# Modulation sums moved from TensorE to VectorE, ScalarE and GpSimd in a two-layer token trunk

## The chip, the core and the metric

The kernel runs on one core of one Trainium2 chip. The metric is the device time of one execution in microseconds (us). Three executions of the kernel before took 2267.44, 2270.04 and 2270.38 us, a median of 2270.04 us.

## The reference: what is computed

The trunk has two layers. Each layer runs a feed-forward sub-layer (FFN), a token-mixing block and a second FFN, over 256 latent rows and 256 context rows of width 1024. Each sub-layer s of each layer l is modulated by three vectors of 1024 numbers, a shift, a scale and a gate. They are products of SiLU(c) for latents, or SiLU(c_ctx) for context, with one column block of the weight `w_ada[l]` (1024 x 9216), plus a bias. The parts that matter here are:

```
def modulated_norm(xs, gain, mod, s):
    return rms_norm(xs, gain) * (1.0 + mod_vec(mod, 3 * s + 1)) + mod_vec(mod, 3 * s)

def gated_residual(xs, y, gain, mod, s, weight):
    return xs + weight * mod_vec(mod, 3 * s + 2) * rms_norm(y, gain)

def ffn_sublayer(xs, mod, s, g_pre, g_post, w_in_f, w_out_f):
    a, g = jnp.split(modulated_norm(xs, g_pre, mod, s) @ w_in_f, 2, axis=-1)
    return gated_residual(xs, (jax.nn.silu(a) * g) @ w_out_f, g_post, mod, s, MACARON_WEIGHT)
```

Only the latent rows leave the trunk. In the second layer the context rows therefore stop mattering after they have given keys, values and states to the mixing block: the gate of its mixing block and all three vectors of its second FFN are read for latents alone. The input x, c, ctx and all weights are float32.

## The kernel before: how the work is laid out

**Main products.** Each float32 operand is split in a high and a low part (`whi`/`wlo` for weights, `hThi`/`hTlo` for activations), and a product is three matmuls, L284 to L286. Weights come in tiles of 1 MB (`wraw`, two buffers). ScalarE copies each half of one into `whi` (L207), VectorE subtracts to get `wlo` (L210), and three such pairs are buffered. In the mixing block GpSimd takes over L210.

**An FFN** (`ffn`) has two parts. The input products run over 44 blocks of 24 matmuls of 512 columns. After a block ScalarE applies SiLU (L654), or VectorE multiplies (L658), ScalarE copies (L660) and VectorE subtracts (L661). The output products follow in `natural_out`. There are four FFNs. The first (layer 0), the second (layer 0, after mixing) and the third (layer 1) carry modulation work beside their input products. The fourth carries none.

**Modulation sums** (`Ada`). Before, a vector takes four chunks of 256 rows by 1024 columns of `w_ada` (1 MB each, L319), which lie in turn in two tiles, `adaG` and `aday`. A chunk is used by four float32 matmuls of 32 rows (L340), two for each of its two 128-row blocks, that go to four 32-row strips of one PSUM tile. After four chunks ScalarE copies the sums out (L346). For a shift or scale, four transposes (L291) and VectorE additions of the bias (L362 to L365) finish the vector. For a gate, four matmuls with a selection matrix `sel` (L381) join the partial sums, VectorE adds the bias and multiplies the gains (L383, L384), and a small DMA from GpSimd's queue writes it to DRAM (L387), from where `load_gate` spreads it over all rows.

**Order of work.** Instructions are emitted in program order into each engine's queue, and each engine runs its own queue in that order. Modulation work is a generator. The main code calls `tick` with a nominal time, twice per block with 2.6. The generator runs one step at a tick if its wake time has passed, and a step says when it wants to wake (`every`). In the three FFNs that carry it, the input products give 88 ticks. After the last block `finish(K, ada)` runs every step that is left, one after the other, before anything of the output products is emitted. Chunk DMAs stand on the queue of SyncE (SP), in one line with the loads of `wraw`, and the DMA of a chunk waits until its place has been read.

Of the kernel before, what the change touches and what calls it, by code (L numbers as in the profile page):

```python
# [297 lines left out]
def aux_tile(K):  # L298
    return K.ps_aux.tile([P, 512], F32, tag="aux", name="aux")


def t2k(K, name="t2k"):
    return K.tp.tile([P, 512], F32, tag="t2k", name=name)


class Ada:


    def __init__(self, K, places, jobs):

        self.K, self.places, self.jobs = K, places, jobs
        self.chunks = [(l, c, k) for l, s, kind, _ in jobs
                       for c in ((3 * s, 3 * s + 1) if kind == "norm" else (3 * s + 2,)) for k in range(0, 8, 2)]
        self.loaded = self.n = 0
# [8 lines left out]
    def run(self, every, bank=aux_tile):  # L323
        self.every, self.bank = every, bank
        self.pump()
        yield every[0]
        for l, s, kind, weight in self.jobs:
            yield from (self.norm(l, s) if kind == "norm" else self.gate(l, s, weight))

# [37 lines left out]

    def gate(self, l, s, weight):

        K, nc, v, q = self.K, self.K.nc, self.K.nc.vector, self.K.nc.gpsimd  # L370
        c0 = (3 * s + 2) * D
        ev = yield from self.sums()
        bp = t2k(K, "bp")
        v.memset(bp, 0.0)
        for st in range(2):
            nc.sync.dma_start(bp[st:st + 97:32, 0:256], K.b_ada[l, c0:c0 + D].rearrange("(q c) -> q c", q=4))
            nc.sync.dma_start(bp[st:st + 97:32, 256:512], K.norm_post[l, s].rearrange("(q c) -> q c", q=4))
        yield 8.0
        pt = self.bank(K)
        for k in range(4):  # L380
            nc.tensor.matmul(pt[32 * k:32 * k + 32, 0:256], K.sel[:, k // 2, :], ev[:, 256 * (k % 2):256 * (k % 2) + 256], start=True, stop=True,  # L381
                             tile_position=(0, 32 * k))
        v.tensor_tensor(out=ev[:, :256], in0=pt[:, :256], in1=bp[:, 0:256], op=OP.add)  # L383
        v.scalar_tensor_tensor(out=ev[:, :256], in0=ev[:, :256], scalar=weight, in1=bp[:, 256:512], op0=OP.mult, op1=OP.mult)  # L384
        gd = K.dr.tile([2, 4, 256], F32, tag=f"gd{l}{s}", name=f"gd{l}{s}")
        for st in range(2):
            q.dma_start(gd[st], ev[st:st + 97:32, :256])  # L387
        K.gd[l, s] = gd
# [232 lines left out]

def ffn(K, l, s, f, pn, tiles, nxt, jobs, every=(5.0, 7.6), pools=None, prep=False):
    nc = K.nc
# [7 lines left out]
    with pools.es as es:  # L631
        hb = None
        big = [gp.tile([P, 2, 1024], F32, tag=t, name="ada" + t) for t in ("G", "y1")]
        ada = add_task(K, Ada(K, big, jobs).run(every), 5.0)
        hid = lambda k, n: (ha[k][:, n, :] if n < 11 else hb[k][:, n - 11, :])
# [51 lines left out]
        G = gp.tile([P, 2, 1024], F32, tag="G", name="G")  # L687
        load_gate(K, l, s, G)
        y1 = gp.tile([P, 4, 512], F32, tag="y1", name="y1")
# [930 lines left out]
def trace(K, nc, tc, rec):  # L1620
# [4 lines left out]
    with ExitStack() as es:  # L1625
# [17 lines left out]
        K.sc = C([P, 8, 32], "sc")  # L1643
        K.sel = C([P, 2, 32], "sel")
        K.npT = C([P, 2, 3, 8], "npT")
# [13 lines left out]
        nc.scalar.activation(K.sc[:, :, 0:2], pt[:, 0:16].rearrange("p (s b) -> p b s", s=2), AF.Silu)  # L1659
        nc.vector.memset(K.sel, 0.0)  # L1660
        id4 = K.ident.rearrange("p (a b r) -> p a b r", a=2, b=2)
        nc.vector.tensor_tensor(out=K.sel[:, :, 0:2], in0=id4[:, 0, :, 0:2], in1=id4[:, 1, :, 0:2], op=OP.add)
        pt = aux_tile(K)
# [5 lines left out]
        for l in range(2):  # L1669
# [5 lines left out]
        ada = Ada(K, [h[:, 4 * j:4 * j + 4, :].rearrange("p (i a) b -> p i (a b)", i=2) for h in pools.hidden(F32) for j in range(2)],  # L1675
                  [(0, 0, "norm", None)])
        for i, _ in enumerate(ada.run((0.0, 0.0), mm_tile)):
# [24 lines left out]
        for l in range(2):  # L1702
            last = l == 1
            jobs = [(0, 0, "gate", 0.5), (0, 1, "norm", None), (0, 1, "gate", 1.0)] if l == 0 else []
            jobs.append((l, 2, "norm", None))
            if last:
                jobs.append((l, 2, "gate", 0.5))
            pn = ffn(K, l, 0, 0, pn, range(4), lambda: PreNorm(K, l, 1), jobs, (7.6, 7.6) if last else (5.0, 7.6), pools, True)
            pools = None
            pn = mix(K, l, pn, last, lambda: PreNorm(K, l, 2))  # L1710
            if last:
                ffn(K, l, 2, 1, pn, range(2), None, [])
            else:
                pn = ffn(K, l, 2, 1, pn, range(4), lambda: PreNorm(K, l + 1, 0), [(l, 2, "gate", 0.5)] + [(l + 1, i, *j) for i, w in ((0, 0.5), (1, 1.0)) for j in (("norm", None), ("gate", w))])

# [64 lines left out]
```

## Time and profile of the kernel before

| | |
|---|---|
| median of three executions | 2270.04 us |
| profiled execution | 2264.31 us, span 2262.5 us |
| mean granted TensorE clock | 0.982 |
| TensorE matmul busy | 2150.5 us (95%) |
| VectorE busy | 1123.5 us (50%) |
| ScalarE busy | 770.1 us (34%) |
| GpSimd busy | 400.0 us (18%) |
| DMA | 323.12 MB, mean 143 GB/s |

In the profile PE is TensorE's matmul side and PEld its weight loads. DVE is VectorE, ACT ScalarE, POOL GpSimd and SP SyncE. A line such as L340 is a line of the kernel before. Times are in us unless marked ns. Matmuls are pipelined, so the busy time of one is longer than the distance to the next, and the distance between starts is what counts. The profiled execution is 1.8 us longer than its span.

### The profile page before, as it was taken

To read this page: it belongs to the slowest core of one execution; us is meant where nothing else is said; L and a number is where in the kernel's file an instruction comes from. 1 tells how busy PE (TensorE), PEld (TensorE's weight loads), DVE (VectorE), ACT (ScalarE), POOL (GpSimd) and SP (SyncE) were. 2 spreads that over 40 slices of the span, in tenths; PEclk is the share of its full clock that TensorE was granted. 3 is DMA by queue.
4 is the path that set the end of the run, shared out by engine and by line. 5 is a ranking of instruction groups with operands and counts; after the bars stand their busy time and mean duration, and the time that the engine had idled before them with its cause. 6 is when DMAs were issued, how large, how long until landed. Compare 5 with 4: busy or idle time off the path is not lost.

```text
span 2262.5 us, 29051 instructions
## 1 busy us (share of the span) xinstructions
PE 2150.5 (95%) x11691; PEld 1731.5 (77%) x11691; DVE 1123.5 (50%) x2025; ACT 770.1 (34%) x1287; POOL 400.0 (18%) x372
## 2 busy tenths in 40 slices
PE   5899999989999999999999988999999889897998
PEld 3677778877777678777777876778887778787997
DVE  6883332357446655532332356733324675646554
ACT  3222222333532433422222332222223345344443
POOL 1660000022313110100000027500000243441000
PEclk8999999999999999999999998999999999998999
DMA  8566542333312122355554335633332553333554
GB/s 292 177 221 211 188 153 88 108 131 134 115 51 82 47 89 93 120 197 177 183 186 156 110 116 170 228 132 112 103 103 87 184 168 104 120 123 130 187 182 154
DMA packets 210910, 323.12 MB, mean 143 GB/s; under 512 B 15608, under 2 KB 152440, under 8 KB 210776
## 3 DMA queue, kind: packets, MB, share of 16 engines
q1 hardware_dynamic: 196736, 287.17, 38.1%
q0 software_dynamic: 9584, 31.56, 4.2%
q10 hardware_dynamic: 4456, 2.53, 0.4%
q8 instruction: 92, 1.51, 0.3%
q14 instruction: 42, 0.34, 0.0%
HBM read 307.57 MB, written 14.71 MB: 142 GB/s over the span
## 4 chain that ended last, share of the span: by engine, by line
PE 48%; DVE 5%; issue 1%; ACT 1%; POOL 1%; DMA 1%; ACTq 0%; SPq 0%; DVEq 0%; POOLq 0%
PE mm L284 15%; PE mm L285 14%; PE mm L286 14%; PE aux L340 2%; PE aux L291 1%; PE aux L1398 1%; DMA r_tq<-tab 1%; DVE wlo L210 1%; ACT jk L399 0%; DVE hThi L461 0%; PE aux L1548 0%; ACT h L458 0%; DVE hTlo L462 0%; DVE xs L432 0%; PE aux L1604 0%
## 5 line engine op out<-in xcount | busy, mean ns | idle before, releaser
L284 PE MATMUL mm<-hThi,whi 128*128 128x512 f32 (+1 forms) x1992 | 719.1, 361 | 8.4 <-DVE hThi L461 8.2
L285 PE MATMUL mm<-hTlo,whi 128*128 128x512 f32 (+1 forms) x1992 | 702.4, 353 | 7.5 <-POOL hTlo L462 7.1
L286 PE MATMUL mm<-hThi,wlo 128*128 128x512 f32 (+1 forms) x1992 | 700.0, 351 | 0.0
L210 DVE TENSOR_TENSOR wlo<-wraw,whi 128x1024 fp32r<-128x1024 f32 (+1 forms) x285 | 362.7, 1278 | 427.8 <-ACT whi L207 426.3
L284 PEld LDWEIGHTS mm<-hThi,whi 128*128 128x128 f32 x1992 | 381.3, 191 | 124.9 <-issue 54.5
L207 ACT ACTIVATE whi<-wraw 128x1024 fp32r<-128x1024 f32 (+1 forms) x348 | 363.7, 1048 | 237.9 <-PE mm L286 174.8
L285 PEld LDWEIGHTS mm<-hTlo,whi 128*128 128x128 f32 x1992 | 381.2, 191 | 59.4 <-POOL hTlo L462 10.1
L286 PEld LDWEIGHTS mm<-hThi,wlo 128*128 128x128 f32 x1992 | 380.9, 191 | 50.3
L210 POOL TENSOR_TENSOR wlo<-wraw,whi 128x1024 fp32r<-128x1024 f32 (+1 forms) x66 | 162.8, 2472 | 898.7 <-ACT whi L207 860.2
L658 DVE TENSOR_TENSOR sa<-sa,mm 128x512 f32<-128x512 f32 (+1 forms) x88 | 54.4, 618 | 160.2 <-PE mm L286 160.2
L654 ACT ACTIVATE sa<-mm 128x512 f32<-128x512 f32 (+1 forms) x88 | 47.8, 543 | 228.2 <-PE mm L286 228.2
L284 PE MATMUL mm<-whi,ha 128*128 128x512 f32 x308 | 120.0, 389 | 0.0
L285 PE MATMUL mm<-wlo,ha 128*128 128x512 f32 x308 | 119.9, 389 | 0.0
L286 PE MATMUL mm<-whi,ha 128*128 128x512 f32 x308 | 119.8, 389 | 0.0
L660 ACT ACTIVATE ha<-sa 128x512 fp32r<-128x512 f32 (+1 forms) x44 | 25.4, 578 | 228.9 <-DVE sa L658 228.9
L660 ACT ACTIVATE hb<-sa 128x512 fp32r<-128x512 f32 (+1 forms) x44 | 25.4, 578 | 178.3 <-DVE sa L658 169.7
L284 PE MATMUL mm<-whi,hThi 128*128 128x512 f32 (+2 forms) x224 | 81.9, 366 | 3.4 <-DVE hThi L461 3.4
L286 PE MATMUL mm<-whi,hTlo 128*128 128x512 f32 (+2 forms) x224 | 80.7, 360 | 4.4 <-POOL hTlo L462 4.3
L285 PE MATMUL mm<-wlo,hThi 128*128 128x512 f32 (+2 forms) x224 | 80.2, 358 | 1.2 <-DVE wlo L210 1.2
L387 POOL DMA_DIRECT2D gd<-ev x12 | 7.0, 583 | 414.6 <-ACT whi L207 253.4
L284 PE MATMUL mm<-whi,hb 128*128 128x512 f32 x188 | 73.1, 389 | 0.0
L285 PE MATMUL mm<-wlo,hb 128*128 128x512 f32 x188 | 73.1, 389 | 0.0
(445 smaller groups left out, 2976.8 us busy)
## 6 DMA issues: line engine op xcount, KB each, us to landing
wraw<-in_w_ffn_in_dram SPq DMA_DIRECT2D x88, 1024.0 KB
wraw<-in_w_in_dram SPq DMA_DIRECT2D x42, 1024.0 KB
wraw<-in_w_ffn_out_dram SPq DMA_DIRECT2D x40, 1024.0 KB
adaG<-in_w_ada_dram SPq DMA_DIRECT2D x32, 1024.0 KB
aday<-in_w_ada_dram SPq DMA_DIRECT2D x32, 1024.0 KB
ha<-in_w_ada_dram SPq DMA_DIRECT2D x8, 1024.0 KB
braw<-in_w_branch_dram SPq DMA_DIRECT2D x32, 256.0 KB
wraw<-in_w_out_dram SPq DMA_DIRECT2D x7, 1024.0 KB
```

The lines of the kernel that those rows point to most:

```text
L207: K.nc.scalar.activation(h3, r, AF.Copy)
L210: (self.eng or K.lo_eng).tensor_tensor(out=l3, in0=r, in1=h3.bitcast(F32), op=OP.subtract)
L284: mm(out, ahi, bhi, start=first, stop=False)
L285: mm(out, ahi, blo, start=False, stop=False)
L286: mm(out, alo, bhi, start=False, stop=last)
L291: K.nc.tensor.transpose(out, x, K.ident[:n, :n])
L340: nc.tensor.matmul(ps[o:o + 32, :], self.K.sc[:, k + i, :], w[:, i, 512 * b:512 * b + 512], start=k == 0, stop=k == 6, tile_position=(0, o))
L387: q.dma_start(gd[st], ev[st:st + 97:32, :256])
L654: nc.scalar.activation(sa[:, :N], ps[:, :N], AF.Silu)
L658: nc.vector.tensor_tensor(out=g[:, :N], in0=g[:, :N], in1=ps[:, :N], op=OP.mult)
L660: nc.scalar.activation(hh, g[:, :N], AF.Copy)
L1398: nc.tensor.matmul(p[64 * (k % 2):64 * (k % 2) + 64, :P], vf(t, h, kb), tl[:, P * kb:P * kb + P], start=kb == 0, stop=kb == nk // P - 1)
```

## The change

The vectors of the three FFNs are summed in another way (`AdaSum`), all but the two of layer 0's mixing norm, which keep `Ada` and come first in the first FFN. A chunk is now 128 rows by 512 columns of `w_ada` (256 KB). Four places for chunks lie in the tile that was `adaG`, and the tile that was `aday` holds accumulators of 128 x 1024 for latents and for context.

For each chunk VectorE multiplies it by the column of SiLU(c) for its rows, one number per partition, and adds it to the latent accumulator (L399, or L397 for the first row block). For context, ScalarE multiplies the chunk in place (L401), and GpSimd adds it to the context accumulator (L403). The chunk's place is free after that. A vector is 16 such steps.

After the 16 steps the sums over partitions are float32 matmuls with a matrix of ones, two for latents and two for context (`total`, L421). Then the vector goes on much as before. The selection matrix and its matmuls are gone. Four vectors are made for latents alone (`ns` = 1), without L401 and L403: the gate of layer 1's mixing block and the three vectors of layer 1's second FFN. The same `w_ada` bytes are read as before.

In the first FFN `AdaSum` makes 4 vectors, after the 2 by `Ada`: the gates of that FFN and of layer 0's mixing block, and the shift and scale of layer 0's second FFN. The second FFN makes 7 vectors, the last with latents alone, and the third makes 3 with latents alone. `every` is 1.6 in the first two and 3.2 in the third.

```
+    def run(self, every):
...
+        for l, s, kind, weight, ns in self.jobs:
+            for k in range(8):
+                for b in range(2):
+                    w = self.places[self.n % len(self.places)]
+                    a = [self.acc[:, st, 512 * b:512 * b + 512] for st in range(2)]
+                    f = [self.K.sc[:, k, st:st + 1] for st in range(2)]
+                    if k == 0:
+                        nc.vector.tensor_scalar(out=a[0], in0=w, scalar1=f[0], scalar2=None, op0=OP.mult)
+                    else:
+                        nc.vector.scalar_tensor_tensor(out=a[0], in0=w, scalar=f[0], in1=a[0], op0=OP.mult, op1=OP.add)
+                    if ns > 1:
+                        nc.scalar.activation(w if k else a[1], w, AF.Copy, scale=f[1])
+                        if k:
+                            nc.gpsimd.tensor_tensor(out=a[1], in0=a[1], in1=w, op=OP.add)
+                    self.n += 1
+                    self.pump()
+                    if k == 7 and b == 1 and kind == "gate":
+                        rows = self.rows(l, s, ns)
+                    yield every
+            yield 2.5
...
+    def total(self, ns):
+        ps = aux_tile(self.K)
+        for st in range(ns):
+            for b in range(2):
+                o = 64 * st + 32 * b
+                self.K.nc.tensor.matmul(ps[o:o + 32, :], self.K.ones[:, 0:32], self.acc[:, st, 512 * b:512 * b + 512], start=True, stop=True,
+                                        tile_position=(0, o))
...
-        ada = add_task(K, Ada(K, big, jobs).run(every), 5.0)
+
+        def modulation():
+            if first:
+                yield from Ada(K, big, first).run((5.0, 7.6))
+            yield from AdaSum(K, [big[0][:, j // 2, 512 * (j % 2):512 * (j % 2) + 512] for j in range(4)], big[1], jobs).run(every)
+
+        ada = add_task(K, modulation(), 5.0)
...
             if last:
-                jobs.append((l, 2, "gate", 0.5))
+                jobs, first, every = [*norm(1, 2, 1), (1, 2, "gate", 0.5, 1)], (), 3.2
+            else:
+                jobs, first, every = [(0, 0, "gate", 0.5, 2), (0, 1, "gate", 1.0, 2), *norm(0, 2, 2)], ((0, 1),), 1.6
...
+                jobs = [(l, 2, "gate", 0.5, 2)]
+                for i, w in ((0, 0.5), (1, 1.0)):
+                    jobs += [*norm(l + 1, i, 2), (l + 1, i, "gate", w, 2 - i)]
+                pn = ffn(K, l, 2, 1, pn, range(4), lambda: PreNorm(K, l + 1, 0), jobs)
```

Code that is not changed stands 80 to 86 lines lower in the changed kernel (L658 is L744 there, L661 is L747, L536 is L616). Two places show how the queues change. First, TensorE's queue where the second FFN's input products end (`mm<-hThi`) and its output products begin (`mm<-whi,ha`). Before:

```order
L284 MATMUL mm<-hThi,whi 128x512
L285 MATMUL mm<-hTlo,whi 128x512
L286 MATMUL mm<-hThi,wlo 128x512
L340 MATMUL aux<-adaG,sc 32x512 x4
L340 MATMUL aux<-aday_7247,sc 32x512 x4
L381 MATMUL aux<-ev,sel 32x256 x4
L284 MATMUL mm<-whi,ha_7244 128x512
L285 MATMUL mm<-wlo,ha_7244 128x512
```

And in the changed kernel at the same place:

```order
L285 MATMUL mm<-hTlo,whi 128x512
L286 MATMUL mm<-hThi,wlo 128x512
L421 MATMUL aux<-aday_7418,ones 32x512 x4
L291 MATMUL aux<-ident,ev 128x128 x4
L421 MATMUL aux<-aday_7418,ones 32x512 x4
L291 MATMUL aux<-ident,ev 128x128 x4
L421 MATMUL aux<-aday_7418,ones 32x512 x2
L284 MATMUL mm<-whi,ha_7415 128x512
```

Two chunks and the selection of one gate stood between the two products. Now the ends of three vectors stand there, and no main product between them.

Second, VectorE's queue at the same place (`sa<-sa,mm` and `hb` are the last blocks' results, `aday` the accumulators, `ba` the gate's bias, `wlo` the next weights). Before:

```order
L658 TENSOR_TENSOR sa<-sa,mm 128x512
L661 TENSOR_TENSOR hb_8112<-sa,hb_8111 128x512
L374 MEMSET bp 128x512
L383 TENSOR_TENSOR ev<-aux,bp 128x256
L384 SCALAR_TENSOR_TENSOR ev<-ev,bp 128x256
L210 TENSOR_TENSOR wlo<-wraw,whi 128x1024 x9
```

And in the changed kernel:

```order
L744 TENSOR_TENSOR sa<-sa,mm 128x512
L747 TENSOR_TENSOR hb_8344<-sa,hb_8343 128x512
L399 SCALAR_TENSOR_TENSOR aday_7418<-adaG,sc,aday_7418 128x512 x4
L442 TENSOR_TENSOR mB<-aux,bT 128x4x2x2
L397 TENSOR_SCALAR aday_7418<-adaG,sc 128x512 x2
L399 SCALAR_TENSOR_TENSOR aday_7418<-adaG,sc,aday_7418 128x512 x14
L442 TENSOR_TENSOR mA<-aux,bT 128x4x2x2
L444 TENSOR_TENSOR mA<-mA,npT 128x16
L397 TENSOR_SCALAR aday_7418<-adaG,sc 128x512 x2
L399 SCALAR_TENSOR_TENSOR aday_7418<-adaG,sc,aday_7418 128x512 x14
L463 TENSOR_TENSOR ba<-aux,ba 64x512
L464 SCALAR_TENSOR_TENSOR ba<-ba,np 64x512
```

Of the second FFN's 112 steps, 36 (4 + 16 + 16) stand behind the last block's results. At the same place of the first FFN 14 of 64 steps stand there, and in the third 8 of 48.

## Rows read from the trace of the kernel before

**Rows 1.** Busy time of each engine in the three input-product stretches (windows).

```profile
core 0: us, PE busy (x) PEld busy (x) DVE busy (x) ACT busy (x) POOL busy (x), PEclk, DMA share, GB/s
54.00:335.00 281.00, 269.81 (x1407) 201.41 (x1406) 148.00 (x277) 74.72 (x102) 76.16 (x85) 0.98 0.55 188
950.00:1241.00 291.00, 288.91 (x1399) 214.65 (x1392) 93.45 (x111) 77.56 (x100) 4.54 (x8) 1.00 0.54 183
1367.00:1640.00 273.00, 269.24 (x1349) 211.55 (x1348) 138.08 (x203) 75.72 (x101) 68.85 (x78) 0.99 0.46 153
```

**Rows 2.** The same windows, instructions of L340 alone, their sum.

```profile
sum 845.00, PE 67.60 PEld 10.32; mean PE 22.53 PEld 3.44
```

**Rows 3.** Timeline around one chunk (start, duration, engine).

```profile
1099.81 0.39 PE L286 MATMUL mm<-hThi,wlo 128*128 128x512 f32 x1
...
1100.12 1.06 PE L340 MATMUL aux<-aday,sc 128*32 128x512 f32 x8
...
1101.12 0.50 PE L284 MATMUL mm<-hThi,whi 128*128 128x512 f32 x1
...
1101.46 0.39 PE L285 MATMUL mm<-hTlo,whi 128*128 128x512 f32 x1
...
1101.69 0.39 PE L286 MATMUL mm<-hThi,wlo 128*128 128x512 f32 x1
...
1101.81 1.23 DVE L210 TENSOR_TENSOR wlo<-wraw,whi 128x1024 fp32r<-128x1024 f32 x1 [4.21 <-ACT whi L207]
```

**Rows 4.** Timeline where the second FFN's input products end.

```profile
1212.88 1.06 PE L340 MATMUL aux<-adaG,sc 128*32 128x512 f32 x8
...
1215.33 1.07 PE L340 MATMUL aux<-aday,sc 128*32 128x512 f32 x8 [1.38 <-DMA aday<-in_w_ada_dram]
```

**Rows 5.** The chain of waits there, in order of time.

```profile
1210.07 5.22 DMA aday<-in_w_ada_dram
...
1216.46 0.60 ACT ev L346
...
1217.11 0.64 PE aux L381 x8
```

**Rows 6.** A block's results on VectorE and ScalarE, timeline.

```profile
1106.90 0.69 DVE L658 TENSOR_TENSOR sa<-sa,mm 128x512 f32<-128x512 f32 x1 [3.32 <-PE mm L286]
...
1107.62 0.63 ACT L660 ACTIVATE hb<-sa 128x512 fp32r<-128x512 f32 x1 [5.36 <-DVE sa L658]
...
1108.28 0.69 DVE L661 TENSOR_TENSOR hb<-sa,hb 128x512 fp32r<-128x512 f32 x1 [0.70 <-ACT hb L660]
```

**Rows 7.** Single operations, by line: durations ns min/median/max, first and last start.

```profile
L511 DVE SCALAR_TENSOR_TENSOR x<-z,po_rst,x x20: 751/752/754, 445.8 to 2258.1; 128x512 f32<-128x512 f32 x20
...
L462 POOL TENSOR_TENSOR hTlo<-h,hThi x22: 1262/1274/1387, 37.3 to 2069.6; 128x512 fp32r<-128x512 f32 x22
L462 DVE TENSOR_TENSOR hTlo<-h,hThi x22: 691/693/1647, 38.9 to 2068.5; 128x512 fp32r<-128x512 f32 x22
...
L104 POOL TENSOR_TENSOR p_xr<-p_px,p_B x8: 1048/1058/2371, 79.4 to 1436.3; 128x512 f32<-128x512 f32 x8
```

**Rows 8.** VectorE beside GpSimd in the mixing block, timeline.

```profile
781.17 2.36 POOL L210 TENSOR_TENSOR wlo<-wraw,whi 128x1024 fp32r<-128x1024 f32 x1 [10.73 <-ACT whi L207]
781.55 2.52 DVE L881 TENSOR_TENSOR mrg<-mrg,sg 128x512 f32<-128x512 f32 x1
```

**Rows 9.** Four transposes of a vector, timeline of the second FFN.

```profile
1199.02 0.60 PE L291 MATMUL aux<-ident,ev 128*128 128x128 f32 x4
```

**Rows 10.** What SP's DMA queue waited for in the second FFN.

```profile
SPq L319 <- PE aux L340: 116.6, 19, 8.9
```

**Rows 11.** Windows of 40 us: start of the third FFN, and one after gaps.

```profile
1360.00:1400.00 40.00, 39.58 (x234) 31.55 (x235) 32.13 (x68) 14.05 (x21) 28.03 (x26) 0.93 0.45 153
1400.00:1440.00 40.00, 36.24 (x211) 27.23 (x210) 30.92 (x50) 8.67 (x13) 34.17 (x40) 0.91 0.57 180
2040.00:2080.00 40.00, 27.71 (x161) 24.77 (x161) 27.18 (x44) 18.18 (x37) 11.28 (x7) 0.83 0.31 106
```

More of the change, by code (lines that the diff above doesn't have):

```diff
@@ L311, in __init__ @@
         self.K, self.places, self.jobs = K, places, jobs
-        self.chunks = [(l, c, k) for l, s, kind, _ in jobs
-                       for c in ((3 * s, 3 * s + 1) if kind == "norm" else (3 * s + 2,)) for k in range(0, 8, 2)]
+        self.chunks = [(l, c, k) for l, s in jobs for c in (3 * s, 3 * s + 1) for k in range(0, 8, 2)]
         self.loaded = self.n = 0
@@ L326, in run @@
         yield every[0]
-        for l, s, kind, weight in self.jobs:
-            yield from (self.norm(l, s) if kind == "norm" else self.gate(l, s, weight))
+        for l, s in self.jobs:
+            yield from self.norm(l, s)
     def sums(self):
@@ L619, in __init__, with ffn @@
             self.ptask = add_task(K, s5_prep(K, l, pp, K.tab[l], self.loads))
-def ffn(K, l, s, f, pn, tiles, nxt, jobs, every=(5.0, 7.6), pools=None, prep=False):
+def ffn(K, l, s, f, pn, tiles, nxt, jobs, every=1.6, pools=None, prep=False, first=()):
     nc = K.nc
@@ L687, in ffn @@
         G = gp.tile([P, 2, 1024], F32, tag="G", name="G")
-        load_gate(K, l, s, G)
+        load_gate(K, l, s, G, nt // 2)
         y1 = gp.tile([P, 4, 512], F32, tag="y1", name="y1")
@@ L1643, in trace @@
         K.sc = C([P, 8, 32], "sc")
-        K.sel = C([P, 2, 32], "sel")
+        K.ones = C([P, 64], "ones")
         K.npT = C([P, 2, 3, 8], "npT")
@@ L1659, in trace @@
         nc.scalar.activation(K.sc[:, :, 0:2], pt[:, 0:16].rearrange("p (s b) -> p b s", s=2), AF.Silu)
-        nc.vector.memset(K.sel, 0.0)
-        id4 = K.ident.rearrange("p (a b r) -> p a b r", a=2, b=2)
-        nc.vector.tensor_tensor(out=K.sel[:, :, 0:2], in0=id4[:, 0, :, 0:2], in1=id4[:, 1, :, 0:2], op=OP.add)
+        nc.vector.memset(K.ones, 1.0)
         pt = aux_tile(K)
@@ L1675, in trace @@
         ada = Ada(K, [h[:, 4 * j:4 * j + 4, :].rearrange("p (i a) b -> p i (a b)", i=2) for h in pools.hidden(F32) for j in range(2)],
-                  [(0, 0, "norm", None)])
+                  [(0, 0)])
         for i, _ in enumerate(ada.run((0.0, 0.0), mm_tile)):
@@ L1703, in trace @@
             last = l == 1
-            jobs = [(0, 0, "gate", 0.5), (0, 1, "norm", None), (0, 1, "gate", 1.0)] if l == 0 else []
-            jobs.append((l, 2, "norm", None))
+            norm = lambda a, b, ns: [(a, b, "shift", None, ns), (a, b, "scale", None, ns)]
             if last:
-                jobs.append((l, 2, "gate", 0.5))
-            pn = ffn(K, l, 0, 0, pn, range(4), lambda: PreNorm(K, l, 1), jobs, (7.6, 7.6) if last else (5.0, 7.6), pools, True)
+                jobs, first, every = [*norm(1, 2, 1), (1, 2, "gate", 0.5, 1)], (), 3.2
+            else:
+                jobs, first, every = [(0, 0, "gate", 0.5, 2), (0, 1, "gate", 1.0, 2), *norm(0, 2, 2)], ((0, 1),), 1.6
+            pn = ffn(K, l, 0, 0, pn, range(4), lambda: PreNorm(K, l, 1), jobs, every, pools, True, first)
             pools = None
@@ L1713, in trace @@
             else:
-                pn = ffn(K, l, 2, 1, pn, range(4), lambda: PreNorm(K, l + 1, 0), [(l, 2, "gate", 0.5)] + [(l + 1, i, *j) for i, w in ((0, 0.5), (1, 1.0)) for j in (("norm", None), ("gate", w))])
+                jobs = [(l, 2, "gate", 0.5, 2)]
+                for i, w in ((0, 0.5), (1, 1.0)):
+                    jobs += [*norm(l + 1, i, 2), (l + 1, i, "gate", w, 2 - i)]
+                pn = ffn(K, l, 2, 1, pn, range(4), lambda: PreNorm(K, l + 1, 0), jobs)
 def trunk(tc, *args):
```

73 lines of the change are left out of this document (55 added, 18 removed).

## The prediction

> **What bounds the kernel now.** I read first the busy time of each engine in the three stretches that carry the modulation work [rows 1]. TensorE is busy 270 of 281 us, 289 of 291 and 269 of 273, at a granted clock of 0.98 to 1.00. VectorE is busy for 53%, 32% and 51%, ScalarE for 27 to 28%, and GpSimd for 4.5 us in the second stretch. So TensorE bounds these stretches, and the other three have idle time. Next I read what the removed work costs TensorE [rows 2, 3], then what happens at the end of a stretch [rows 4, 5], because there the changed queue has no main product between the last sums. At that end TensorE already waits before: the last chunk's DMA lands 5.22 us after the place was free, TensorE waits 1.38 us for it, then 0.7 us for ScalarE's copy.
>
> **What leaves TensorE.** One chunk delays the main products by 1.2 us: four starts lie between 1099.81 and 1101.69, 1.88 us, and three distances of 0.23 us would be 0.69 [rows 3]. Of 64 chunks in the FFNs, 8 stay, so 56 x 1.19 = 66.6 us go. By busy time alone a chunk is 67.6 / 64 = 1.06 us [rows 2], which gives 59.1. I take the distance and keep the other for the range. Six selections of 0.64 us go (3.8), and the two waits at the second FFN's end (1.4 and 0.7) [rows 4, 5]. Together 72.5 us.
>
> **What comes to TensorE in the stretches.** Of 14 sums with ones, 9 stand among blocks. Seven are four float32 matmuls like a chunk, 7 x 1.19 = 8.3 us. Two are half of that, between 0.6 and 1.2, say 1.0 each. Together 10.3 us. The net saving is 62 us, by the lower price of a chunk 55.
>
> **The new steps inside the stretches.** A block lasts 24 x 0.226 = 5.4 us [rows 3] and holds two steps. VectorE's part of a step I price like its multiply-add of two SBUF operands at the same size, 0.75 us. GpSimd's add is 1.27 us by one such operation, 1.05 by another. ScalarE's multiply is 0.60 [rows 5, 7]. VectorE then has wlo 1.23 [rows 3], half of two block results 0.69 [rows 6] and 1.50 for steps, 3.4 of 5.4 us. GpSimd has 2.5. The cover is that idle time, and the wlo of a block is made two blocks ahead. What this costs if the cover fails is bounded by the case that the two engines never run together: 3.4 + 2.54 = 5.96, which is 0.55 us above a block, over 63 blocks 35 us. In the third FFN the steps are VectorE's alone, but its first 80 us have VectorE at 32 and 31 of 40 us and TensorE with gaps [rows 11]. Some 15 steps of 0.75 us fall in them, 11 us at most. The lower end for both is nothing. I take 5 us, near the lower end, because every wait of an SP load on a chunk's place before (19 times, the longest 8.9 us) left TensorE 99% busy [rows 1, 10]. The new load of a chunk waits for GpSimd's add in the same way, with `wraw` loads behind it.
>
> **The steps that are left at the end of a stretch.** These are on the path. The generator gets 88 ticks and needs more, so 14, 36 and 8 steps stand behind the last block's results, and TensorE's next main product stands behind the sums of these steps. Each tail starts when VectorE has passed sa, ScalarE's copy and hb, 2.1 us after the last matmul [rows 6].
>
> A step with context uses VectorE (0.75), ScalarE (0.60) and GpSimd (1.27) in turn, and the steps follow each other. Does GpSimd's add run beside VectorE's? In the mixing block VectorE's mrg, with two SBUF operands, starts 0.38 us after a GpSimd subtraction, and ends 0.54 us after it, lasting 2.52 us [rows 8], where such an operation takes 0.69 [rows 7]. So it stood still until GpSimd was done. I therefore take the sum, 0.75 + 1.27 = 2.02 us per step. The lower bound is GpSimd alone, 1.27, the upper the way round one of the four places with a load of 5.22 us and one stop of the two engines for each other, (0.75 + 0.60 + 1.27 + 5.22 + 2.02) / 4 = 2.5. There are 32 such steps, 14 in the first FFN and 18 in the second: 64.6 us, bounds 41 and 80. Two more with context write the accumulator first and need no GpSimd, 1.5 us.
>
> The Trainium skill ("SBUF — State Buffer", Who interferes with whom) says that a VectorE instruction with two SBUF inputs contends with a GpSimd instruction that reads SBUF, and that the second to issue is fully blocked. The pair just read agrees. It speaks against the change: without it 32 steps would be 41 us instead of 65.
>
> A step without context is VectorE's 0.75 us if chunks are there, and with a load of 5.22 us for every place (0.75 + 5.22) / 4 = 1.5. The trace has no load of a quarter chunk, so I take 1.2, between the ends and nearer the load. There are 24 such steps (16 in the second FFN, 8 in the third), 28.8 us, bounds 18 and 36.
>
> The same page (The DMA setup-cost knee) gives about 2 us plus bytes over 436 GB/s for one transfer. By that a 256 KB load would take an estimated 2.6 us, these 24 steps about 20 us instead of 29, and the forecast would be 9 us lower. The 1 MB load would be 4.4 us by it and took 5.22, and no run here shows the smaller one.
>
> The joins: a shift or scale in a tail ends with the sum on TensorE (1.07), the copy (0.60) and four transposes (0.60) [rows 4, 5, 9], with gaps 2.5 us, three times. A gate ends with the sum alone, 1.07, twice.
>
> So the first FFN's tail is 2.1 + 28.3 + 2.5 = 32.9 us, the second's 2.1 + 36.4 + 1.5 + 19.2 + 5.0 + 1.1 = 65.3, the third's 2.1 + 9.6 + 1.1 = 12.8: 111 us in all, bounds 76 and 134. In the row where TensorE is busy 27.7 of 40 us its granted clock averages 0.83 [rows 11]: 6.8 us of full clock are missing, granted at the lower level (1.2 GHz), a part of them in the idle time itself. So a long wait also costs clock after it, between nothing and half of that, 3.4 us. I take 2 us for each tail, 6.
>
> **The sum.** 111 + 6 + 5 - 62 = 60 us more than before. The profiled execution took 2264.3 us (span 2262.5), so it would take 2324. It lies 5.7 us under the median of the runs, and against that median the forecast is 2330 us. From the lower ends, 76 - 62 = +14, so 2284. From the upper, 134 + 10 + 35 - 55 = +124, so 2394.
>
> **Rivals.** *Both engines are short inside the stretches too.* If VectorE and GpSimd stop each other at each step, the 35 us above replace the 5, wlo comes late block after block, and the time is 2360. For it: the stop in [rows 8]. Against: only operations with two SBUF operands would stop, and two blocks' weights lie ready.
>
> *The saving wins.* The tails cost less than the 62 us saved when a step averages under (62 - 17.4) / 58 = 0.77 us, where 17.4 is the entries and joins. That needs GpSimd's add to keep VectorE's pace, with no stop and the chunks always there. At 0.75 a step the tails are 61 us, and with no loss of clock the time is 2269. A gain would need a saving above the 62 as well. For it: chunks are preloaded and GpSimd is idle otherwise. Against: no GpSimd operation of this size is under 1.05 us [rows 7].
>
> *The loads of weights come late.* If a `wraw` load stands behind two chunk loads that each wait a full step of 2 us more than before, TensorE loses 4 us at each of some 30 weight tiles, 120 us, and the time is 2450. Against: such waits of up to 8.9 us were hidden before [rows 10].
>
> **Chances.** The forecast with its bounds 0.77, the shortage inside the stretches 0.12, the saving wins 0.08, late weights 0.03. The range 2286 to 2378 leaves out the last two and the top of the bounds. A measurement of this kernel can tell 0.2%, 4.5 us, from no change. Slower by more: 0.92. Within: 0.04, and faster: 0.04, both from the case that the saving wins.
>
> **What would show it.** In the profile after, L340 must fall to 8 chunks in the FFNs. TensorE should have three gaps of about 33, 65 and 13 us where the input products end, ended by L421 waiting for GpSimd's add or VectorE, with L399 and L403 alternating at about 2.0 us a step. Inside the stretches TensorE should stay above 97% busy. The forecast is wrong if the gaps add up to less than 62 us, or if TensorE waits for wlo or `wraw` inside the stretches.

## The result

The changed kernel takes 2324.31 us (median of 4 runs, 2323.08 to 2326.19), the kernel before 2269.14 on the same chip. The ratio is 1.0244, 95% interval 1.0227 to 1.0262: slower by 55 us. The forecast was 2330, with a range of 2286 to 2378. The profiled execution took 2326.19 us, span 2324.4, where 2324 had been worked out for it.

Windows of the profile after; the columns are those of [rows 1].

```profile
core 0: us, PE busy (x) PEld busy (x) DVE busy (x) ACT busy (x) POOL busy (x), PEclk, DMA share, GB/s
1040.00:1080.00 40.00, 40.00 (x182) 32.17 (x181) 23.90 (x28) 19.64 (x28) 13.50 (x11) 1.00 0.58 185
320.00:360.00 40.00, 17.17 (x70) 10.61 (x70) 23.40 (x25) 16.67 (x24) 23.80 (x16) 0.73 0.49 150
1200.00:1240.00 40.00, 12.86 (x42) 6.16 (x40) 25.27 (x28) 18.01 (x26) 29.00 (x20) 0.73 0.53 160
1240.00:1280.00 40.00, 23.34 (x78) 13.46 (x79) 17.25 (x25) 5.11 (x6) 6.86 (x8) 0.71 0.49 159
1440.00:1480.00 40.00, 29.05 (x144) 22.45 (x144) 33.14 (x57) 6.42 (x10) 35.43 (x36) 0.83 0.46 145
```

In the middle of the second FFN (first row) TensorE is as full as in [rows 1], with VectorE at 24 of 40 us. The next three rows are the ends of the first and the second FFN: TensorE works 13 to 23 of 40 us, at a granted clock of 0.71 to 0.73. The last row lies in the S5 preparation of the third FFN, where TensorE also has gaps. (The S5 preparation is work for the mixing block that the first and the third FFN carry on VectorE, GpSimd and TensorE beside their input products.)

The prediction wanted TensorE above 97% busy inside the stretches. From the first SiLU to the last input product of each FFN it was:

```profile
61.30:333.70 272.40, 258.51 (x1279) 202.75 (x1278) 175.10 (x298) 104.74 (x147) 133.07 (x127) 0.97 0.57 184
974.20:1206.60 232.40, 232.40 (x1054) 188.94 (x1052) 145.61 (x167) 116.99 (x164) 87.14 (x73) 1.00 0.58 182
1413.00:1678.30 265.30, 249.47 (x1193) 201.14 (x1192) 160.37 (x234) 70.83 (x95) 68.79 (x74) 0.96 0.46 149
```

That is 95%, 100% and 94%. The windows of [rows 1] had 96%, 99% and 99%, so the third FFN, and a little the first, fell short. L340 (L339 there) is down to 8 chunks in the FFNs, as it had to be.

What TensorE does at the end of the second FFN, where [rows 4, 5] had two chunks and a selection (timeline of the profile after):

```profile
1205.78 0.39 PE L284 MATMUL mm<-hThi,whi 128*128 128x512 f32 x1
...
1211.67 3.50 PE L421 MATMUL aux<-aday,ones 128*32 128x512 f32 x4 [5.06 <-DVE aday L399]
...
1240.40 5.78 PE L421 MATMUL aux<-aday,ones 128*32 128x512 f32 x8 [21.19 <-DVE aday L399]
...
1263.10 2.52 PE L421 MATMUL aux<-aday,ones 128*32 128x512 f32 x4 [15.57 <-DVE aday L399]
1265.54 0.80 PE L284 MATMUL mm<-whi,ha 128*128 128x512 f32 x1
```

From the last input product, which ends some 0.8 us behind the start of its first row here, to the first output product (L284 with `ha`) lie 59 us. The other two ends have gaps of 30 and 11 us. In the list of waits the sums cost TensorE most (line, releaser, us in total, times, longest):

```profile
PE aux L421 <- DVE aday L399: 73.6, 5, 22.8
PE aux L291 <- POOL p_xr L106: 23.5, 3, 10.0
...
PE mm L286 <- DVE wlo L210: 4.3, 2, 3.6
```

The last of these rows is new. Both of its waits lie in the third FFN's S5 preparation, and a wait of TensorE for `wlo` inside a stretch was one of the prediction's signs of being wrong.

And the steps in that gap (timeline, rows of VectorE and ScalarE):

```profile
1225.23 0.72 ACT L401 ACTIVATE adaG<-adaG,sc 128x512 f32<-128x512 f32 x1 [0.95 <-DVE aday L399]
1225.72 1.15 DVE L399 SCALAR_TENSOR_TENSOR aday<-adaG,sc,aday 128x512 f32<-128x512 f32 x1 [0.53 <-DMA adaG<-in_w_ada_dram]
1226.90 0.72 ACT L401 ACTIVATE adaG<-adaG,sc 128x512 f32<-128x512 f32 x1 [0.95 <-DVE aday L399]
1227.32 1.22 DVE L399 SCALAR_TENSOR_TENSOR aday<-adaG,sc,aday 128x512 f32<-128x512 f32 x1 [0.45 <-DMA adaG<-in_w_ada_dram]
...
1228.99 1.22 DVE L399 SCALAR_TENSOR_TENSOR aday<-adaG,sc,aday 128x512 f32<-128x512 f32 x1 [0.45 <-DMA adaG<-in_w_ada_dram]
```

A step with context comes every 1.67 us, not every 2.02, and each begins with a wait for the DMA of its own quarter chunk. From 1222 to 1246 us a load takes 2.6 us from issue to landing (first row), and 14 loads waited for GpSimd's add before they were issued (second row):

```profile
adaG<-in_w_ada_dram SPq DMA_DIRECT2D x14, 256.0 KB, 2.6
```

```profile
SPq L383 <- POOL aday L403: 18.0, 14, 2.2
```

So the steps wait for loads, and the loads for steps. That was the first hint that neither engine sets the pace. The groups by line (count, busy us and mean ns, idle before and releaser) answer to [rows 7]:

```profile
L403 POOL TENSOR_TENSOR aday<-aday,adaG 128x512 f32<-128x512 f32 x140 | 188.8, 1372 | 234.7 <-ACT adaG L401 234.7
L399 DVE SCALAR_TENSOR_TENSOR aday<-adaG,sc,aday 128x512 f32<-128x512 f32 x196 | 152.0, 806 | 19.9 <-DMA adaG<-in_w_ada_dram 19.9
```

Both are near what single operations took before, 1.27 and 0.75 us.

### The profile page after: what moved, and what is told of

It reads as the page before. It is cut to its first block, busy times and chain, and to the rows that moved or that the text cites. A ratio compares the mean times of both kernels' runs of the same rounds, so it can differ in the third digit from the quotient of the medians.

```text
span 2324.4 us, 29492 instructions
## 1 busy us (share of the span) xinstructions
PE 2124.4 (91%) x11291; PEld 1731.1 (74%) x11291; DVE 1296.5 (56%) x2234; ACT 874.7 (38%) x1441; POOL 600.9 (26%) x521
## 4 chain that ended last, share of the span: by engine, by line
PE 75%; DVE 12%; DMA 4%; POOL 4%; issue 3%; ACT 3%; ACTq 0%; SPq 0%; DVEq 0%; POOLq 0%
PE mm L284 22%; PE mm L286 22%; PE mm L285 22%; PE aux L291 2%; PE aux L1484 2%; DVE wlo L210 2%; DMA r_tq<-tab 1%; PE aux L421 1%; POOL aday L403 1%; DMA adaG<-in_w_ada_dram 1%; PE aux L1634 1%; PE aux L1690 1%; ACT jk L479 1%; DVE hThi L541 1%; ACT h L538 1%
## 5 line engine op out<-in xcount | busy, mean ns | idle before, releaser
L284 PE MATMUL mm<-hThi,whi 128*128 128x512 f32 (+1 forms) x1992 | 715.9, 359 | 4.9 <-DVE hThi L541 4.7
L210 DVE TENSOR_TENSOR wlo<-wraw,whi 128x1024 fp32r<-128x1024 f32 (+1 forms) x285 | 377.9, 1331 | 377.7 <-ACT whi L207 376.2
L284 PEld LDWEIGHTS mm<-hThi,whi 128*128 128x128 f32 x1992 | 381.7, 192 | 87.0 <-issue 31.3
L403 POOL TENSOR_TENSOR aday<-aday,adaG 128x512 f32<-128x512 f32 x140 | 188.8, 1372 | 234.7 <-ACT adaG L401 234.7
L399 DVE SCALAR_TENSOR_TENSOR aday<-adaG,sc,aday 128x512 f32<-128x512 f32 x196 | 152.0, 806 | 19.9 <-DMA adaG<-in_w_ada_dram 19.9
L401 ACT ACTIVATE adaG<-adaG,sc 128x512 f32<-128x512 f32 x140 | 97.7, 724 | 150.7 <-DVE aday L399 150.7
L284 PE MATMUL mm<-whi,ha 128*128 128x512 f32 x308 | 121.3, 394 | 0.0
L421 PE MATMUL aux<-aday,ones 128*32 128x512 f32 x96 | 31.6, 732 | 74.2 <-DVE aday L399 73.6
L744 DVE TENSOR_TENSOR sa<-sa,mm 128x512 f32<-128x512 f32 (+1 forms) x88 | 54.4, 618 | 64.5 <-PE mm L286 64.5
L284 PE MATMUL mm<-whi,hThi 128*128 128x512 f32 (+2 forms) x224 | 82.0, 366 | 3.4 <-DVE hThi L541 3.4
```

Of the source, the lines that this page charges most:

```text
L210: (self.eng or K.lo_eng).tensor_tensor(out=l3, in0=r, in1=h3.bitcast(F32), op=OP.subtract)
L284: mm(out, ahi, bhi, start=first, stop=False)
L399: nc.vector.scalar_tensor_tensor(out=a[0], in0=w, scalar=f[0], in1=a[0], op0=OP.mult, op1=OP.add)
L401: nc.scalar.activation(w if k else a[1], w, AF.Copy, scale=f[1])
L403: nc.gpsimd.tensor_tensor(out=a[1], in0=a[1], in1=w, op=OP.add)
L421: self.K.nc.tensor.matmul(ps[o:o + 32, :], self.K.ones[:, 0:32], self.acc[:, st, 512 * b:512 * b + 512], start=True, stop=True, tile_posit ...
```

## The experiments

Each ran beside the kernel before; ratios are to it, with 95% intervals. The kernel before took 2267.0 to 2269.1 us beside them, so a difference between kernels of different experiments is good to some 2 us. The edits are shortened. In the variants with a rate, lines stand one to five lower than in the changed kernel (in the paced one its L421 is L425, its L399 L400, its L403 L404).

**The steps of the tails left out.**

```
-                    if k == 0:
+                    if K.cut: pass          # the same for ScalarE, GpSimd and the load
+                    elif k == 0:
...
+        K.cut = True
         finish(K, ada)
```

> The 58 steps that stand behind the last block (14, 36 and 8) and their loads are left out; the sums with ones, copies and transposes of the tails stay. So the modulation vectors of those steps are not computed. Theory A (most of the loss lies in the tails): TensorE's gaps of 29.6, 58.9 and 11.3 us, 99.8 us in all, shrink to the entry and the joins, some 2.1 + 2.5, 2.1 + 6.1 and 2.1 + 1.1, 16 us, and the clock gives back some 4: 2324 - 84 - 4 = 2236 us. Theory B (the steps' time in the tails hides something else that is late anyway, weights or the gate's way through DRAM, or the loss lies inside the stretches): over 2290 us. If A holds, 2236 is still about 29 us above 2269 - 62 = 2207, and that remainder is the cost inside the stretches.

Measured: 2231.41 us, ratio 0.984 (0.9825 to 0.9854). Windows at the ends of the first and the second FFN, which now comes at 1176 us:

```profile
320.00:360.00 40.00, 39.07 (x183) 30.48 (x183) 13.40 (x17) 12.25 (x16) 3.69 (x4) 1.00 0.49 161
1160.00:1200.00 40.00, 38.16 (x169) 27.61 (x168) 18.02 (x21) 14.00 (x19) 12.73 (x13) 1.00 0.49 160
```

TensorE works 38 to 39 of 40 us, at full clock. So the steps of the tails cost 2324.3 - 2231.4 = 93 us (91 if each time is taken against the kernel before that ran beside it), and nothing else was late there. Theory A holds.

**The third FFN's steps behind the S5 preparation.** The pace is now a rate (steps a tick) and a start:

```
-    def run(self, every):
+    def run(self, rate, start=6.0):
...
-                    yield every
+                    credit -= 1.0
+                    while credit < 1.0:
+                        credit += rate
+                        yield 1.6
...
-  [*norm(1, 2, 1), (1, 2, "gate", 0.5, 1)], (), 3.2
+  [*norm(1, 2, 1), (1, 2, "gate", 0.5, 1)], (), (1.0, 75.0)
```

> In the third FFN the 48 steps start 75 us of the scheduler's clock later, at one a tick instead of one every second tick, so that they stand behind most of the S5 preparation and still end before the last block. The work is the same. Theory A (steps among the preparation delay it, some 15 us, and 8 steps stand in the tail, gap 11.3 us): 2324 - 15 - 9 = 2300 us. Theory B (the preparation's own chain bounds that part, and the time that TensorE saves there only becomes waiting): only the tail goes, 2315 us. Theory C (twice as many steps a block make VectorE late for wlo): 2324 us or more.

Measured: 2299.68 us, 1.0142 (1.0126 to 1.0157), 25 us less than the changed kernel. The SiLU of the third FFN (first and last start), of the changed kernel, then of this one:

```profile
L740 ACT ACTIVATE sa<-mm x22: 577/598/607, 1413.0 to 1667.5; 128x512 f32<-128x512 f32 x22
```

```profile
L744 ACT ACTIVATE sa<-mm x22: 579/598/607, 1408.5 to 1653.1; 128x512 f32<-128x512 f32 x22
```

254.5 us became 244.6, so 10 us lie inside the stretch, where theory A had 15, and the tail and the clock behind it make the rest. Steps among the preparation were not free.

**Paced so that no tail is left.**

```
-  first FFN 1.6   second 1.6   third 3.2       (us between steps, a tick is 2.6)
+  (1.45,)         (1.75,)      (0.62,)         (steps a tick)
```

> Same work, but 1.45, 1.75 and 0.62 steps a tick in the three FFNs instead of 1, 1 and 0.5, so that all steps end before the last block and no tail is left. Theory A (the tail is a matter of the pace alone): the gaps go (99.8 us less about 5 of entry), five joins of 1.1 us move among the blocks, the clock gives back 4, and 3.5 steps a block load VectorE with 1.23 + 0.69 + 3.5 x 1.13 = 5.9 us of the 5.4 of a block, 0.5 us over some 40 blocks, 20 us: 2324 - 95 + 5 - 4 + 20 = 2250 us. Theory B (VectorE and GpSimd stop each other, so that the faster pace makes every block late): the time of the tails comes back inside the blocks, 2310 us or more.

Measured: 2303.34 us, 1.0156 (1.0141 to 1.0171). Theory A fell: of the 93 us only 21 came back. The waits, a window of the second FFN, and ScalarE and VectorE there:

```profile
PE aux L425 <- DVE aday L400: 30.0, 11, 6.0
...
PE aux L425 <- POOL aday L404: 9.6, 14, 1.3
```

```profile
1040.00:1080.00 40.00, 35.51 (x142) 26.23 (x142) 25.59 (x27) 18.07 (x26) 19.84 (x14) 0.87 0.53 161
```

```profile
1021.54 2.05 ACT L402 ACTIVATE adaG<-adaG,sc 128x512 f32<-128x512 f32 x3 [3.03 <-DVE aday L400]
1023.50 0.58 ACT L744 ACTIVATE sa<-mm 128x512 f32<-128x512 f32 x1
1023.97 1.05 ACT L207 ACTIVATE whi<-wraw 128x1024 fp32r<-128x1024 f32 x1
...
1025.05 1.27 DVE L210 TENSOR_TENSOR wlo<-wraw,whi 128x1024 fp32r<-128x1024 f32 x1 [2.22 <-ACT whi L207]
1026.24 3.10 DVE L400 SCALAR_TENSOR_TENSOR aday<-adaG,sc,aday 128x512 f32<-128x512 f32 x3
```

My own arithmetic for both theories, VectorE's and GpSimd's load, missed it: VectorE is busy only 26 of 40 us. ScalarE waits 3.03 us for VectorE's steps, its `whi` stands behind its multiplies, and VectorE's `wlo` waits 2.22 us for `whi`, with the next steps behind it. Two queues in order hold each other up. That this is what makes the steps late is argued from these rows; the versions below with both sums on VectorE bear it out. TensorE pays at the sums, which wait up to 6.0 us. Behind some of these waits the granted clock is lower too: 0.87 in the window shown.

**The same, with the steps of the first and third FFN behind the preparation.** `(2.0, 36.0)` for the first FFN, `(1.0, 75.0)` for the third.

> As the paced kernel (1.75 steps a tick in the second FFN), but the steps of the first and third FFN start 30 and 69 us of the scheduler's clock later, behind most of the S5 preparation, at 2.0 and 1.0 a tick. Theory A (steps among the preparation cost 7 us in the first FFN and 15 in the third; 4 steps a block behind it load VectorE with 1.92 + 4 x 1.13 = 6.4 us of 5.4, 1.0 us over 16 blocks): 22 less, 16 more than the paced kernel's 2250: 2244 us. Theory B (the preparation is bound by its own chain): no gain from the late start, 2255 to 2270 us.

Measured: 2304.78 us, 1.0168 (1.0147 to 1.0189). At 2.0 steps a tick the first FFN loses in sums what the third gains: its sums wait 23.0 us for VectorE, against 8.3 in the paced kernel. The forecast missed for the same reason as the one before.

**Three places instead of four.** `for j in range(3)` where the changed kernel has `range(4)`.

> Three places for the quarter chunks instead of four; the work and the pace of the scheduler are the same. Theory A (in the tails a step's pace is the way round of one place, about 2.7 us of load, 0.3 of issue, 1.2 on VectorE, 0.7 on ScalarE, 1.4 on GpSimd and gaps, 6.7 us over 4 places = the 1.67 us seen): with three places 2.23 us a step with context and 1.3 us a step without, 32 x 0.56 + 24 x 0.3 = 25 us more than 2324: 2349 us. Theory B (VectorE and GpSimd stop each other, and that sets the 1.67 us): no change, 2324 us.

Measured: 2346.82 us, 1.0348 (1.0333 to 1.0364), 22.5 us more than with four. GpSimd's adds in the second FFN's tail:

```profile
1235.64 1.26 POOL L403 TENSOR_TENSOR aday<-aday,adaG 128x512 f32<-128x512 f32 x1 [1.45 <-ACT adaG L401]
1238.35 2.48 POOL L403 TENSOR_TENSOR aday<-aday,adaG 128x512 f32<-128x512 f32 x2 [1.45 <-ACT adaG L401]
1242.28 1.26 POOL L403 TENSOR_TENSOR aday<-aday,adaG 128x512 f32<-128x512 f32 x1 [1.45 <-ACT adaG L401]
```

Three adds in 1242.28 - 1235.64 = 6.64 us, 2.21 each; with four places four took 4 x 1.67 = 6.7. The way round of one place stays, so it sets the pace. Theory A holds.

**Both sums on VectorE.**

```
-   nc.scalar.activation(w if k else a[1], w, AF.Copy, scale=f[1])
-   if k:
-       nc.gpsimd.tensor_tensor(out=a[1], in0=a[1], in1=w, op=OP.add)
+   if k == 0:
+       nc.vector.tensor_scalar(out=a[1], in0=w, scalar1=f[1], ...)
+   else:
+       nc.vector.scalar_tensor_tensor(out=a[1], in0=w, scalar=f[1], in1=a[1], ...)
```

> VectorE makes the context's sum too, so ScalarE's multiply and GpSimd's add of a step go. Theory A (the way round of a place sets the tail's pace): the round falls to some 4.6 us, 1.15 us a step, then VectorE's own 2 x 0.75 = 1.5 us bounds it, 32 x 0.17 = 5 us less in the tails; inside the stretches VectorE has 1.92 + 2 x 1.5 = 4.9 of 5.4 us, which just holds: 2319 us. Theory B (VectorE at 4.9 of 5.4 us is late for wlo and for the sums block after block): 2335 us or more.

Measured: 2312.95 us, 1.0196 (1.0178 to 1.0214), 11 us less than the changed kernel; I had expected 5. Its tail on VectorE (L404 is the context's sum here):

```profile
1222.71 0.74 DVE L404 SCALAR_TENSOR_TENSOR aday<-adaG,sc,aday 128x512 f32<-128x512 f32 x1
1223.37 0.74 DVE L399 SCALAR_TENSOR_TENSOR aday<-adaG,sc,aday 128x512 f32<-128x512 f32 x1
1224.03 0.74 DVE L404 SCALAR_TENSOR_TENSOR aday<-adaG,sc,aday 128x512 f32<-128x512 f32 x1
```

Starts lie 0.66 us apart, so a step is 1.33 us, against 1.67 with three engines: 32 x 0.34 = 11. Theory A holds, but VectorE's operations follow each other faster than their durations had said.

**Only what fits.** Shifts and scales of the first two FFNs stay on TensorE; the new sums make their gates, and in the third FFN four vectors behind the preparation.

```
-  [(0,0,"gate"), (0,1,"gate"), *norm(0,2)],          first=((0,1),),          1.6
+  [(0,0,"gate"), (0,1,"gate")],                      first=((0,1), (0,2)),    (1.3,)
-  [(0,2,"gate"), norms and gates of (1,0), (1,1)],                            1.6
+  [(0,2,"gate"), (1,0,"gate")],                      first=((1,0), (1,1)),    (1.3,)
-  [*norm(1,2), (1,2,"gate")],                                                 3.2
+  [(1,1,"gate"), *norm(1,2), (1,2,"gate")],                                   (1.5, 75.0)
```

> Only what fits is made by the new sums: the two gates in each of the first two FFNs (1.3 steps a tick, behind the vectors that stay on TensorE), and in the third FFN one gate more, four vectors at 1.5 single steps a tick behind the S5 preparation. Shifts and scales of the first two FFNs stay on TensorE as before. No step is left behind the last block. Theory A (a vector by the new sums saves 4.8 us of chunks and costs about 1.1 us of sum as long as it fits): 8 vectors x 3.7 + 3.8 for the selections = 33 us less than 2267: 2234 us, and some 4 us of late sums: 2238 us. Theory B (each sum with ones stands in TensorE's queue before VectorE is done, as in the paced kernel, 3 us a sum, and the clock falls behind it): 2258 us or more.

Measured: 2248.0 us, 0.9912 (0.9896 to 0.9929), between the two theories.

**The paced kernel with later sums.** Before `total`, `yield 7.6` for `yield 2.5`, and 1.7, 2.1 and 0.65 steps a tick for 1.45, 1.75 and 0.62.

> As the paced kernel, but each sum with ones is issued two ticks (half a block) later behind its vector's last step, and the pace is raised to 1.7, 2.1 and 0.65 steps a tick so that all still fits before the last block. Theory A (the paced kernel lost its time because the sums stood in TensorE's queue while VectorE and GpSimd were behind, 40 us of waits in 25 places, and the clock fell behind these waits): the waits shrink to under 15 us, 2303 - 25 - 10 = 2268 us. Theory B (VectorE, ScalarE and GpSimd just can't do 3.5 to 4 steps a block, so the lag grows and the wait only moves): 2303 us or more.

Measured: 2267.94 us, 0.9998 (0.9988 to 1.0008).

```profile
PE aux L425 <- DVE aday L400: 6.8, 4, 3.6
PE aux L425 <- POOL aday L404: 5.2, 9, 1.1
```

The waits at the sums fell from 39.6 to 12.0 us, the time by 35, although the pace rose. So the place of the sum in TensorE's queue was most of the paced kernel's loss. All 14 vectors by the new sums, without a tail, is just as fast as the kernel before.

**Three versions of the mixed kernel**: late sums (`yield 7.6`), with 1.6, 1.6 and 1.7 steps a tick for 1.3, 1.3 and 1.5; the same with both sums on VectorE; late sums with the first FFN as in the kernel before.

> As the mixed kernel, but each sum with ones stands two ticks later behind its vector's last step, at 1.6, 1.6 and 1.7 steps a tick so that all still ends before the last block. Theory A (in the mixed kernel four blocks with a sum are some 3 us longer than those without, where the sum itself is 1.1 us, because the sum is in TensorE's queue before the accumulators are ready): 4 x 2 = 8 us less than 2248: 2240 us. Theory B (those 3 us are the engines' lag at this pace, whatever the sum's place): 2248 us or more.

> As the kernel before it in this batch, with the context's sum on VectorE too (no ScalarE multiply, no GpSimd add). Theory A (VectorE's load decides: 3.3 steps a block x 1.33 us + 1.92 = 6.3 us of 5.4, over some 20 blocks): 18 us more, 2258 us. Theory B (what decides is the chain VectorE, ScalarE, GpSimd of a step and the wait of wlo for a ScalarE that waits for VectorE; without it blocks lag less): 2240 us or less.

> As the kernel with late sums, but the first FFN makes its modulation vectors as the kernel before does, the gate first, all on TensorE. Only the second and third FFN have the new sums. Theory A (in the changed kernels the first FFN loses some 6 us because GpSimd's p_xr comes 5 us later in the S5 preparation, and that hangs on the order of the vectors there): its length is that of before, 271.5 us from the first to the last SiLU, without the 9.8 us wait for p_xr, and the time is about 2242 us. Theory B (the wait for p_xr hangs on something else): it stays, and the first FFN is some 278 us, the time 2248 us.

Measured: 2247.52 (0.9905, 0.989 to 0.992), 2239.24 (0.9871, 0.9857 to 0.9884) and 2247.75 us (0.9911, 0.9898 to 0.9924). The first did not move, against theory A. The second did, as its theory B had it, against my load of 6.3 us in a block of 5.4. The window at the end of the first FFN, late sums first, then VectorE alone:

```profile
320.00:360.00 40.00, 37.46 (x161) 28.68 (x160) 22.24 (x23) 14.55 (x19) 14.41 (x13) 1.00 0.49 155
```

```profile
320.00:360.00 40.00, 40.00 (x181) 32.19 (x180) 23.57 (x30) 11.02 (x13) 2.19 (x4) 1.00 0.50 165
```

Without the way over ScalarE and GpSimd TensorE is full. In the first of the two windows it had waited 1.2 us for GpSimd's add at a sum and 1.4 us for VectorE's `sa`.

The third version shows what the changed kernel lost in the S5 preparation of the first FFN. An operation of the preparation that stood still, in the timeline of the kernel before, of the changed one, and of this one:

```profile
127.17 7.92 DVE L104 TENSOR_TENSOR p_rt<-p_pr,p_C 128x512 f32<-128x512 f32 x1
```

```profile
123.14 5.94 POOL L105 TENSOR_TENSOR p_F<-p_F,p_sd 128x256 f32<-128x256 f32 x1
```

```profile
126.32 7.39 DVE L102 TENSOR_TENSOR p_cmv<-p_pr,p_C 128x512 f32<-128x512 f32 x1
```

The window around it, of the changed kernel and then of this one:

```profile
120.00:160.00 40.00, 36.09 (x207) 25.41 (x206) 24.23 (x34) 8.94 (x13) 30.26 (x27) 0.91 0.52 172
```

```profile
120.00:160.00 40.00, 40.00 (x273) 29.37 (x268) 32.19 (x35) 11.81 (x18) 25.46 (x30) 1.00 0.69 230
```

With the gate first, VectorE stands and GpSimd runs through; without it, GpSimd stands, its `p_xr` is 5 us later, and TensorE loses 4 us. The first FFN was 272.5 us from its first to its last SiLU, near theory A's 271.5. But the wait of 9.8 us for `p_xr` that theory A wanted gone is still there, as in the kernel before (9.7); what went is a second one, 3.8 us in the changed kernel. And the time did not move: with late sums alone the first FFN already took 271.7 us. In the third version its two gates are on TensorE again, and their eight chunks take back what the preparation gives.

**One vector pair more on VectorE.** In the second FFN `norm(1, 1)` goes over too, and `yield 5.1` stands before `total`.

> As the mixed kernel with both sums on VectorE, but in the second FFN one shift and one scale more go from TensorE to the new sums (four vectors there instead of two, at the same 1.6 steps a tick), and the sums stand one tick earlier. Theory A (a vector saves 4.8 us of chunks and costs 1.1 us of sum while VectorE keeps up; its windows at that pace had VectorE busy 33 to 35 of 40 us and TensorE 40.00): 2 x 3.7 = 7 us less than 2239: 2232 us. Theory B (VectorE at that load for 190 us instead of 90 builds up a lag, and the sums or wlo come late): 2239 us or more.

Measured: 2237.75 us, 0.9868 (0.9851 to 0.9884), not to be told from the 2239. Its second FFN is 3.4 us shorter (238.3 to 234.9 between first and last SiLU), half of the 7; the times are too near each other to show it. VectorE carried the load:

```profile
1080.00:1120.00 40.00, 40.00 (x176) 31.52 (x175) 35.44 (x51) 10.82 (x14) 1.92 (x3) 1.00 0.67 212
```

The two versions with both sums on VectorE beat both kernels, the kernel before by some 1.3%.

## Why the prediction was right, and where its terms were off

*The saving.* A chunk at 1.19 us held. The SiLU of the second FFN, of the kernel before, then of the changed one:

```profile
L654 ACT ACTIVATE sa<-mm x22: 581/597/598, 951.9 to 1199.2; 128x512 f32<-128x512 f32 x22
```

```profile
L740 ACT ACTIVATE sa<-mm x22: 576/580/602, 974.2 to 1196.0; 128x512 f32<-128x512 f32 x22
```

247.3 us from the first to the last became 221.8. From between them 23 chunks and two selections went, and four sums of 1.1 stand there now: 25.5 + 4.4 - 1.3 = 28.6 us for 23 chunks, 1.24 each.

*The steps inside the stretches.* 5 us were forecast. Without the tails the kernel is 36 us under the kernel before; 62 saved, less 5 and less some 10 for the joins, would be 47. So some 16 us were lost here. The cover held in the second FFN, where TensorE had 40.00 of 40 us, and failed in the S5 preparation. The third FFN of the kernel before:

```profile
L654 ACT ACTIVATE sa<-mm x22: 580/598/608, 1368.7 to 1619.1; 128x512 f32<-128x512 f32 x22
```

Twelve chunks and a selection went from these 250.4 us and two half sums came, so some 237.5 should be left; they are 254.5. That is 17 us, where the term, on [rows 11], had 11 at most. 10 of them came back when the steps started later. What the other 7 are stays open; TensorE still waited 8.0 us for `p_xr` there, against 3.7 in the kernel before. In the first FFN, counted in the same way, 7 were lost, 4 of them with the exchanged stop, which was in no term. That the whole is 16 and not 24 is a gain that nobody had forecast, in part at the start of the third FFN: there TensorE waited 5.9 us for `hThi` before and 2.2 after.

*The tails.* Their steps, entry and clock were forecast at 95 + 6 + 6 = 107 us and cost 93. The step that failed is the pace with context. I took VectorE's and GpSimd's durations as a sum, from the stop in [rows 8], 2.02 us. The runs show the way round of one place, 6.65 us, divided by the places: 1.67 with four and 2.21 with three. The stretching of VectorE's operation (1.15 to 1.22 us beside GpSimd, 0.74 without) is one part of that way. The bound of 2.5 had the right mechanism with a load of 5.22 us; the load of a quarter takes 2.6 to 2.7 in the tails (2.9 in the median of the whole kernel). Single steps took 0.99 and 0.93 us instead of 1.2, in the main because the load is shorter. The Trainium skill ("SBUF — State Buffer", Who interferes with whom) says that a VectorE instruction with two SBUF inputs contends with a GpSimd instruction that reads SBUF. The trace agrees as far as VectorE's operation took 1.15 to 1.22 us instead of 0.74, but the two do not add up to the pace of a step. The same page of the Trainium skill (The DMA setup-cost knee) gave an estimated 2.6 us for this load, and the trace agrees with 2.6 to 2.7.

*The clock.* 93 us, less 78 for steps at their measured paces and 6 for the entries, leave 9 for clock and slow joins, against 6. The sum of 5.78 us in the second FFN's tail shows both parts. It is one vector's sum in four matmuls. The first began when half of one accumulator was ready, and GpSimd's last add ended at 1244.28, so 1.9 of the 5.78 us lie behind it. A whole sum among blocks takes 1.07. The granted clock over these 5.78 us was 0.52, nearly all of them at the lower level (1.2 GHz).

So 14 us too much for the tails and 11 too little inside the stretches nearly cancelled. That the sum came out within 2 us of the profiled execution is luck in this respect; the mechanism, tails that outweigh the saving, is not.

*The rivals.* The saving did not win, since 93 us stood against 62. ScalarE's waits for `wraw` loads of `w_in` came to 8.1 us, against 7.3 before, so the weights did not come late. VectorE and GpSimd did not run short in the second FFN at one step a tick, though the paced kernels show that they do, with ScalarE, at 1.75. In the third FFN the sign of that rival, TensorE waiting for `wlo`, did appear, with 4.3 us.

## What to carry to other kernels

Work moved to idle engines pays only as far as it fits beside the bounding engine: count how many steps the generator gets before the stage ends, and leave the rest where it was. Price a loop through several engines by the way round of one buffer divided by the buffers, and ask what each engine's queue holds behind it: VectorE alone, with both sums, beat three engines in turn. Put a dependent instruction of the bounding engine far enough behind its producers, or it stops everything in its queue.

## What the runs showed of the hardware

When VectorE and GpSimd met on operands in SBUF in the S5 preparation, the one that was stopped was not stopped for one instruction of the other but for a whole run of them. A VectorE operation that otherwise took 0.68 us took 7.92 beside six of GpSimd in a row; a GpSimd one took 5.94, and 0.80 in the kernel before, beside seven of VectorE in a row. Which of the two it was changed with the order of the modulation vectors. Yet VectorE came to its run there (`p_cmv`) at nearly the same time in both kernels, 124.88 us before and 124.92 after; what exactly tips it was not taken apart. In the third FFN such a stop held a `wlo` for 8.16 us, where it otherwise took 1.2, and TensorE's 3.6 us wait for `wlo` ended with it. The kernel before has two such stops there (8.05 and 7.46 us) that TensorE did not wait for.

Behind some short waits of TensorE the granted clock fell. In the paced kernel, behind a wait of 4.7 us that ended at 1044.05, it was at the lower level (1.2 GHz), the first row here.

```profile
1044.00:1050.00 6.00, 5.71 (x11) 1.93 (x12) 0.00 (x0) 2.56 (x4) 1.26 (x1) 0.50 0.23 66
1080.00:1120.00 40.00, 35.45 (x150) 26.83 (x151) 24.46 (x28) 19.48 (x28) 22.33 (x15) 1.00 0.58 184
```

It did not fall behind each of them: the second row, also of the paced kernel, holds waits at sums of up to 2.3 us at a clock of 1.00.
